# Twelve ring slots for the small experts' weight loads, and their down weights read in runs of 8192 bytes

## The chip, the cores and the metric

The kernel runs on one core of a Trainium2 chip. The metric is the device time of one execution in microseconds (us); the time before is the median of three runs. Five engines work side by side: TensorE (PE; its weight loads are listed apart as PEld), VectorE (DVE), ScalarE (ACT), GpSimd (POOL) and SyncE (SP), which here issues nearly all transfers. The transfers run on 16 DMA engines of the core.

## The reference

Two layers of a backbone over 256 latent and 256 context tokens of width 1024. Each has a mixer of three parallel head groups; the first ends in a dense SwiGLU, the second in a mixture of eight experts, of which each token takes two. Only that last part matters here:

```
def swiglu(h, wg, wu, wd):
    return (jax.nn.silu(h @ wg) * (h @ wu)) @ wd

def moe_swiglu(h, w_router, wg, wu, wd):            # h (256, 1024), wg, wu (8, 1024, 3584), wd (8, 3584, 1024)
    logits = (t @ w_router).astype(jnp.float32)
    top_v, top_i = lax.top_k(logits, TOP_K)         # TOP_K = 2
    top_w = jax.nn.softmax(top_v, axis=-1)
    gates = jnp.sum(jax.nn.one_hot(top_i, N_EXPERTS) * top_w[..., None], axis=1)
    for e in range(N_EXPERTS):
        y = y + gates[:, e:e + 1] * swiglu(t, wg[e], wu[e], wd[e])
```

Every weight is fp32 and is read once: an expert has three matrices of 14.7 MB, eight experts 352 MB. After the experts come the residual sum and one RMSNorm whose result is the output.

## The kernel before, in words

The mixers and the dense SwiGLU come first. Then the experts run one after the other, `e` = 0 to 7, ordered by how many tokens chose them. The first four (`expert`) hold up to 128 tokens each and multiply in three float32r products: each weight tile is split by ACT and DVE into a high part `eh` (L804) and a low part `el` (L805). The last four, the small experts (`expert_small`, L1235), hold up to 64 tokens and multiply their fp32 weights as they were loaded, with no split.

A small expert goes through its 3584 hidden columns in four chunks of 896 (`FB`; `NB` = 4). One chunk has twelve loads, each a tile of up to 1 MB (128 partitions by up to 2048 fp32):

- eight of gate and up weights, in four pairs (L1268): 256 rows by 896 columns, 896 KB, in runs of 3584 bytes;
- four of down weights (L1257), of the chunk before: three of 256 rows by 1024 columns, one of 128 rows. Row `r0 + k*128 + p` of the matrix goes to partition `p`, so a run is one row, 4096 bytes.

After each pair PE multiplies (L1274; the halves of the columns for gate and up stand in different partitions of `ps`). After the eighth load ACT and DVE make `g = silu(gate) * up` (L1284, L1285); in the next chunk PE transposes `g` seven times, 128 columns at a time (`g_Ts`, L1246), and multiplies it with the down weights into `pd` (L1261). At the end of an expert (`t1`, L1298, which runs inside the next expert's first chunk) `pd` is scaled by DVE (L1313), sent back to its tokens by four products (`py`, L1318) and added to `xtk` (L1322).

Where a load goes is set by a ring of tiles ("slots"): `slot32` (L1066) takes the next name of `ring`, drops a name for good once the load's number has passed its `until`, and puts the name at the end. In the small experts five names are left: `w`, `c`, `r0`, `r1`, `r2`. SP issues the loads in program order, one `dma_start` each (L1232), and holds each until the slot's last reader on PE is done, so at most five loads are under way or waiting to be read. The order of the instructions on each engine is set by a scheduler when the kernel is built; `tc.keep_in_program_order` pins one.

Tiles that the change uses: `mpr` (two buffers each for the tags `wh` and `wl`) and `mpc` (one each) hold the split parts `eh` and `el` of the big experts, whose last two tiles are split within the first small chunk; `xeL1` holds the low part of the tokens of experts 0 and 1. `pgu` is the PSUM pool of `ps`, tags `pg` and `pu`, of two banks each; `pmt` has two banks that the transposes and `py` share.

The last expert gets `end=square` (L1389): after its additions DVE and ACT compute the squares' sums and `x * g_final` (L1337), and `finish` (L1343) scales and stores the result.

```
    ring = ["w", "c", "r0", "r1", "xh", "xl", "xt", "y", "r2", "xc"]                              # L913
    until = {"xc": 36, "xt": 42, "y": 42, "xh": 62, "xl": 62}                                     # L914
    nm = ring.pop(0)                                                                              # L1070
    while i >= until.get(nm, i + 1):                                                              # L1071
```

Of the kernel before, what the change touches and what calls it, by code (L numbers as in the profile page):

```python
# [11 lines left out]
F32 = mybir.dt.float32  # L12
# [8 lines left out]
P = 128  # L21
# [70 lines left out]
def hybrid_backbone_kernel(  # L92
# [41 lines left out]
    def bank(pool, name):  # L134
        return pool.tile([P, 512], F32, tag="b", name=name)
# [754 lines left out]
    for k in range(KD):  # L890
# [13 lines left out]

    slots = {"w": lambda: mpw.tile([P, 2048], F32, tag="w32", name="e32"),
             "c": lambda: mpc.tile([P, 2048], F32, tag="w32", name="e32"),
             "xh": lambda: mp.tile([P, 2048], F32, tag="xeH0", name="e32"),
             "xl": lambda: mp.tile([P, 2048], F32, tag="xeL0", name="e32"),
             "xt": lambda: mp2.tile([P, 2048], F32, tag="xtk", name="e32"),
# [88 lines left out]
    def half(ap):  # L998
        return ap.rearrange("p (a n) -> p a n", n=NL)
# [226 lines left out]
    def load_raw(dram, kk, n):  # L1226
        i = n_load[0]
        n_load[0] += 1
        w32 = slot32(i)
        assert len(w32.shape) == 2  # L1230
        wv = w32[:, :kk * n].rearrange("p (k n) -> p k n", n=n)
        nc.sync.dma_start(wv, dram)  # L1232
        return wv

    def expert_small(xs, wg, wu, wd, e, tail, hooks, end=None):  # L1235
        H = P // 2
        xv = xs[:, :, (e - NBIG) * H:(e - NBIG + 1) * H]
        pd = [None]

        HB = FB // 2  # L1240
        NB = FE // FB

        def g_Ts(g):
            pt = bank(pmt, "pgt")
            for q in range(FK):
                nc.tensor.transpose(pt[:, q * H:(q + 1) * H], g[0:H, q * P:(q + 1) * P], ident[0:H, 0:H])  # L1246
            gt = mp2.tile([P, FK, H], F32, tag="gts", name="gts")
            copy_bal(gt, pt[:, 0:FK * H].rearrange("p (q n) -> p q n", n=H))
            return gt

        def down_s(gt, j):
            if pd[0] is None:
                pd[0] = pdn.tile([P, 512], F32, tag=f"pd{e % 2}", name="pds")
            for q0 in range(0, FK, 2):
                kn = min(2, FK - q0)
                r0 = j * FB + q0 * P
                w = load_raw(wd[r0:r0 + kn * P, :].rearrange("(k p) n -> p k n", p=P), kn, D)  # L1257
                for k in range(kn):
                    q = q0 + k
                    for o in range(2):  # L1260
                        mm(pd[0][H * o:H * o + H, :], lhsT=gt[:, q, :], rhs=w[:, k, o * 512:(o + 1) * 512],  # L1261
                           start=j == 0 and q == 0, stop=j == NB - 1 and q == FK - 1, skip_group_check=True)

        prev = None
        for j in range(NB):
            ps = pgu.tile([P, 2, 512], F32, tag=("pg", "pu")[j % 2], name="pgs")
            for c in range(KD // 2):
                ws = [load_raw(w_ap[c * 256:(c + 1) * 256, j * FB:(j + 1) * FB].rearrange("(k p) n -> p k n", p=P), 2, FB)  # L1268
                      for w_ap in (wg, wu)]
                for k in range(2):  # L1270
                    kk = 2 * c + k
                    for b in range(2):
                        for o in range(2):
                            mm(ps[H * o:H * o + H, b, 0:HB], lhsT=xv[:, kk, :], rhs=ws[o][:, k, b * HB:(b + 1) * HB],  # L1274
                               start=kk == 0, stop=kk == KD - 1, skip_group_check=True)
                if c == 1:
                    if prev is not None:
                        gt = g_Ts(prev)
# [12 lines left out]
            for f in (hooks or {}).get(j, ()):  # L1291
                f()
        last = []

        def t0():
            last.append(g_Ts(prev))

        def t1():  # L1298
            if end:
                tc.keep_in_program_order(nc.scalar.preload_act_table_set(LN_EXP))  # L1300
                new_xg()
            down_s(last[0], NB - 1)
            pt = bank(pmt, "pst")
            for t in range(2):
                nc.tensor.transpose(pt[:, t * P:(t + 1) * P], f32(S[:, t, e, :]), ident)
            for t in range(2):
                mm(pt[:, 256:257], lhsT=f32(S[:, t, e, :]), rhs=gatp[:, t, e:e + 1], start=t == 0, stop=t == 1)
            ST = mp2.tile([P, 256], F32, tag="ST", name="STs", bufs=2)
            nc.vector.tensor_copy(ST, pt[:, 0:256])
            gs = mp.tile([P, 1], F32, tag="gs", name="gs", bufs=2)  # L1310
            nc.vector.tensor_copy(gs, pt[:, 256:257])
            yo = part(y32, e % 2)
            stt(yo, half(pd[0]), gs, ga2s, op0=ALU.mult, op1=ALU.mult)  # L1313
            for t in range(2):
                pys = []
                for o in range(2):
                    py = bank(pmt, "py")
                    mm(py, lhsT=ST[H * o:H * o + H, t * P:(t + 1) * P], rhs=yo[H * o:H * o + H], start=True, stop=True)  # L1318
                    pys.append(py)
                for o in range(2):  # L1320
                    cs = slice(o * 512, (o + 1) * 512)
                    tt(xtk[:, t, cs], xtk[:, t, cs], pys[o], ALU.add)  # L1322
            if end:
                for o in range(2):
                    end(o)
        return t0, t1

    xg = None
# [5 lines left out]
    ssq4 = mp.tile([P, 2, 2], F32, name="ssq4")  # L1334
    junk = xT[:, 4:6, 0:NL]

    def square(o):  # L1337
        for t in range(2):
            xo = half(xtk[:, t, o * 512:(o + 1) * 512])
            act(junk, xo, AF.Square, accum_out=ssq4[:, t, o:o + 1])  # L1340
            tt(half(xg[:, t, o * 512:(o + 1) * 512]), xo, part(gfb, o), ALU.mult)

    def finish():  # L1343
        tt(ssq, ssq4[:, :, 0], ssq4[:, :, 1], ALU.add)
# [37 lines left out]
    for e in range(NE):  # L1382
        if e == 0:
            ws = [w[0, 0] for w in (wm_g, wm_u, wm_d)]
        else:
            ws = [w[0, ds(which[e], 1)].rearrange("o a b -> (o a) b") for w in (wm_g, wm_u, wm_d)]
        hooks = {j: f for (ee, j), f in plan.items() if ee == e}
        if e >= NBIG:
            tail = expert_small(xes[NBIG], *ws, e, tail, hooks, square if e == NE - 1 else None)  # L1389
            continue  # L1390
        xe, h = (x01, e * P) if e < 2 else (xes[2], (e - 2) * P)
        xv = (xe[0][:, :, h:h + P], xe[1][:, :, h:h + P])
        gt_ = gates if e == 0 else gatp
        tail = expert(xv, *ws, lambda t, e=e: S[:, t, e, :], lambda t, e=e, g=gt_: g[:, t, e:e + 1], tail, hooks, e == 0)
    tail[0]()
    tail[1]()
    finish()

    cv = nc.values_load(cnti[0:1, 0:1], min_val=0, max_val=NL)
    with tc.If(cv > 0):  # L1400
        pc = mp3.tile([P, 2], F32, name="pc")
        gc = mp3.tile([P, 2], F32, name="gc")
        bc = mp3.tile([P, 1], F32, name="bc")
        S2 = mp3.tile([P, 2, P], F32R, name="S2")
        xe2 = xe_tiles(1)
        for blk in range(2):
            with tc.For_i(0, NE, 1) as ei:
                nc.vector.tensor_copy(pc, posm[:, :, ds(ei, 1)].rearrange("p t o -> p (t o)"))
                nc.vector.tensor_copy(gc, gates[:, :, ds(ei, 1)].rearrange("p t o -> p (t o)"))
                nc.vector.tensor_copy(bc, base[:, ds(ei, 1)])  # L1410
                ts_(pc, pc, bc, float(P * blk), op0=ALU.subtract, op1=ALU.subtract)
# [8 lines left out]
        for o in range(2):  # L1420
            square(o)
        finish()


# [29 lines left out]
```

## Time and profile before

| | |
|---|---|
| median of 3 runs | 1977.64 us (1975.27 to 1979.37) |
| the profiled execution | 1976.52 us, of which its span is 1974.7 us |
| PE busy | 1816.8 us, 92% |
| PEld busy | 1259.1 us, 64% |
| DVE busy | 979.2 us, 50% |
| ACT busy | 758.7 us, 38% |
| read from memory | 477.39 MB, 242 GB/s over the span |

The shares are means over stages with different limits. The page shows the span in 40 slices of 49.4 us; the small experts are the last ten or so. There PE is busy eight tenths of the time and DVE hardly at all, while the DMA engines stand at nine tenths or more. A DMA share is the mean busy share of the 16 engines; a packet counts as busy from its start to its end, and packets can overlap, so a share can come out a little over 1.

### The profile page before, as it was taken

To read this page: it belongs to the slowest core of one execution; us is meant where nothing else is said; L and a number is where in the kernel's file an instruction comes from. 1 tells how busy PE (TensorE), PEld (TensorE's weight loads), DVE (VectorE), ACT (ScalarE), POOL (GpSimd) and SP (SyncE) were. 2 spreads that over 40 slices of the span, in tenths; PEclk is the share of its full clock that TensorE was granted. 3 is DMA by queue.
4 is the path that set the end of the run, shared out by engine and by line. 5 is a ranking of instruction groups with operands and counts; after the bars stand their busy time and mean duration, and the time that the engine had idled before them with its cause. 6 is when DMAs were issued, how large, how long until landed. Compare 5 with 4: busy or idle time off the path is not lost.

```text
span 1974.7 us, 23529 instructions
## 1 busy us (share of the span) xinstructions
PE 1816.8 (92%) x9280; PEld 1259.1 (64%) x9280; DVE 979.2 (50%) x1294; ACT 758.7 (38%) x965; POOL 46.7 (2%) x75
## 2 busy tenths in 40 slices
PE   7998999999999999999899999999998878887876
PEld 4756766778877887777687878888785322222222
DVE  5474555633333345755678888988984101010101
ACT  3424454422222224345566777777662000000001
POOL 1030000000000000210000000000000000000000
PEclk8999999999999999999989999999999999999998
DMA  8765243342334334553489789999998999999996
GB/s 281 223 178 143 70 132 100 115 144 70 101 99 156 110 108 155 158 140 128 146 298 360 255 305 330 334 356 361 353 340 317 366 388 388 388 382 402 396 397 249
DMA packets 261922, 480.05 MB, mean 243 GB/s; under 512 B 11630, under 2 KB 141996, under 8 KB 261804
## 3 DMA queue, kind: packets, MB, share of 16 engines
q1 hardware_dynamic: 259296, 474.19, 67.8%
q0 software_dynamic: 1312, 2.62, 0.9%
q10 hardware_dynamic: 1196, 1.66, 0.3%
q8 instruction: 75, 1.23, 0.3%
q14 instruction: 43, 0.35, 0.1%
HBM read 477.39 MB, written 1.05 MB: 242 GB/s over the span
## 4 chain that ended last, share of the span: by engine, by line
PE 74%; DMA 15%; DVE 7%; ACT 3%; issue 2%; SPq 0%; POOL 0%; DVEq 0%; ACTq 0%; POOLq 0%
DMA e<-in_w_moe_up_dram 10%; PE pd L1146 8%; PE pgs L1274 6%; DMA e<-in_w_moe_down_dram 3%; PE pu L152 3%; PE pg L151 3%; PE pu L153 3%; PE pg L152 3%; PE pu L151 3%; PE pg L153 2%; PE pds L1261 2%; PE psg L151 2%; PE psu L151 2%; PE psu L152 2%; PE psu L153 2%; PE psd L151 2%
## 5 line engine op out<-in xcount | busy, mean ns | idle before, releaser
L805 DVE TENSOR_TENSOR el<-e,eh 128x2048 fp32r<-128x2048 f32 (+1 forms) x173 | 375.4, 2189 | 49.5 <-ACT eh L804 48.8
L804 ACT ACTIVATE eh<-e 128x2048 fp32r<-128x2048 f32 (+1 forms) x173 | 316.7, 1839 | 93.1 <-PE pu L153 32.7
L1274 PE MATMUL pgs<-e,xs 128*64 128x448 f32 x1024 | 228.7, 557 | 71.1 <-DMA e<-in_w_moe_up_dram 64.4
L1274 PEld LDWEIGHTS pgs<-e,xs 128*64 128x64 f32 x1024 | 75.6, 138 | 218.7 <-DMA e<-in_w_moe_up_dram 105.0
L144 ACT ACTIVATE wh<-w 128x2048 fp32r<-128x2048 f32 (+2 forms) x70 | 125.4, 1791 | 208.4 <-issue 80.0
L145 DVE TENSOR_TENSOR wl<-w,wh 128x2048 fp32r<-128x2048 f32 (+2 forms) x70 | 149.6, 2138 | 97.9 <-ACT wh L144 97.9
L1285 DVE TENSOR_TENSOR es<-es,pgs 64x448 f32<-64x448 f32 x32 | 19.9, 623 | 324.0 <-ACT es L1284 324.0
L1284 ACT ACTIVATE es<-pgs 64x448 f32<-64x448 f32 x32 | 17.2, 537 | 325.6 <-PE pgs L1274 315.2
L1261 PE MATMUL pds<-e,gts 128*64 128x512 f32 x448 | 109.6, 599 | 9.9 <-DMA e<-in_w_moe_down_dram 9.0
L151 PE MATMUL pg<-eh,xeH 128*128 128x512 f32 x224 | 89.7, 400 | 0.6 <-ACT eh L804 0.6
L151 PE MATMUL psp<-hH,wh 128*128 128x512 f32 (+1 forms) x224 | 86.7, 391 | 3.1 <-ACT hH L276 3.0
L152 PE MATMUL pg<-el,xeH 128*128 128x512 f32 x224 | 89.4, 399 | 0.0
L151 PE MATMUL pu<-eh,xeH 128*128 128x512 f32 x224 | 88.8, 397 | 0.0
L152 PE MATMUL pu<-el,xeH 128*128 128x512 f32 x224 | 88.2, 394 | 0.7 <-DVE el L805 0.6
L151 PE MATMUL psq<-wh,hH 128*128 128x256 f32 x304 | 88.5, 291 | 0.0
L153 PE MATMUL pg<-eh,xeL 128*128 128x512 f32 x224 | 88.5, 395 | 0.0
L152 PE MATMUL psq<-wl,hH 128*128 128x256 f32 x304 | 87.7, 289 | 0.0
L153 PE MATMUL pu<-eh,xeL 128*128 128x512 f32 x224 | 87.7, 391 | 0.0
L153 PE MATMUL psq<-wh,hL 128*128 128x256 f32 x304 | 87.4, 287 | 0.0
L152 PE MATMUL psp<-hL,wh 128*128 128x512 f32 (+1 forms) x224 | 86.1, 384 | 0.0
L153 PE MATMUL psp<-hH,wl 128*128 128x512 f32 (+1 forms) x224 | 85.6, 383 | 0.0
L1261 PEld LDWEIGHTS pds<-e,gts 128*64 128x64 f32 x448 | 32.0, 136 | 68.6 <-issue 39.0
(504 smaller groups left out, 3470.8 us busy)
## 6 DMA issues: line engine op xcount, KB each, us to landing
e<-in_w_moe_down_dram SPq DMA_DIRECT2D x103, 1024.0 KB, 7.9
e<-in_w_moe_gate_dram SPq DMA_DIRECT2D x64, 896.0 KB, 7.8
e<-in_w_moe_up_dram SPq DMA_DIRECT2D x64, 896.0 KB, 7.1
e<-in_w_moe_gate_dram SPq DMA_DIRECT2D x55, 1024.0 KB, 7.3
e<-in_w_moe_up_dram SPq DMA_DIRECT2D x55, 1024.0 KB, 6.5
wmod<-in_w_mod_dram SPq DMA_DIRECT2D x96, 512.0 KB, 5.7
w<-in_w_in_dram SPq DMA_DIRECT2D x24, 1024.0 KB, 8.0
w<-in_w_ffn_gate_dram SPq DMA_DIRECT2D x11, 1024.0 KB, 5.8
```

The costliest lines, as they stand in the source:

```text
L144: act(wh[:, :m], w32[:, :m], AF.Copy)
L145: tt(wl[:, :m], w32[:, :m], f32(wh[:, :m]), ALU.subtract)
L151: mm(ps, lhsT=sh, rhs=mh, start=first, stop=False)
L152: mm(ps, lhsT=sh, rhs=ml, start=False, stop=False)
L153: mm(ps, lhsT=sl, rhs=mh, start=False, stop=last)
L804: act(h3[:, b], w[:, b], AF.Copy)
L805: tt(l3[:, b], w[:, b], f32(h3[:, b]), ALU.subtract)
L1146: mm(pds[o], lhsT=gt[sh][:, q, :], rhs=w[mh][:, k, o * 512:(o + 1) * 512], start=a and j == 0 and q == 0, stop=z and j == NJ - 1 and q == 3)
L1261: mm(pd[0][H * o:H * o + H, :], lhsT=gt[:, q, :], rhs=w[:, k, o * 512:(o + 1) * 512], start=j == 0 and q == 0, stop=j == NB - 1 and q == F ...
L1274: mm(ps[H * o:H * o + H, b, 0:HB], lhsT=xv[:, kk, :], rhs=ws[o][:, k, b * HB:(b + 1) * HB], start=kk == 0, stop=kk == KD - 1, skip_group_c ...
L1284: act(gv, ps[0:H, b, 0:HB], AF.Silu)
L1285: tt(gv, gv, ps[H:P, b, 0:HB], ALU.mult)
```

## The change

The ring gets seven more names as the first small expert (`e == NBIG`) starts its second chunk: the two buffers of each of `wh` and `wl` in `mpr`, the two of `mpc`, and `xeL1`. Ring order then is the five old names and the seven new ones. Within the down weights' loads a partition now takes seven rows in sequence (row `p*7 + k` of the chunk), so two rows are one run of 8192 bytes in memory; the fourth load, with one row, keeps 4096. The columns of `g` are transposed in the matching order, every seventh column. In the last expert the four products `py` go to the `pgu` banks, and the additions come before the products with `g_final`. After the experts the ring goes back to five names for code that does not run with these inputs.

```
--- before.py
+++ after.py
@@ -904,6 +904,11 @@
 
     slots = {"w": lambda: mpw.tile([P, 2048], F32, tag="w32", name="e32"),
              "c": lambda: mpc.tile([P, 2048], F32, tag="w32", name="e32"),
+             "mh": lambda: mpr.tile([P, 2048], F32, tag="wh", name="e32"),
+             "ml": lambda: mpr.tile([P, 2048], F32, tag="wl", name="e32"),
+             "ch": lambda: mpc.tile([P, 2048], F32, tag="wh", name="e32"),
+             "cl": lambda: mpc.tile([P, 2048], F32, tag="wl", name="e32"),
+             "xm": lambda: mp.tile([P, 2048], F32, tag="xeL1", name="e32"),
              "xh": lambda: mp.tile([P, 2048], F32, tag="xeH0", name="e32"),
              "xl": lambda: mp.tile([P, 2048], F32, tag="xeL0", name="e32"),
              "xt": lambda: mp2.tile([P, 2048], F32, tag="xtk", name="e32"),
@@ -1243,7 +1248,7 @@
         def g_Ts(g):
             pt = bank(pmt, "pgt")
             for q in range(FK):
-                nc.tensor.transpose(pt[:, q * H:(q + 1) * H], g[0:H, q * P:(q + 1) * P], ident[0:H, 0:H])
+                nc.tensor.transpose(pt[:, q * H:(q + 1) * H], g.rearrange("p (n k) -> p k n", k=FK)[0:H, q], ident[0:H, 0:H])
             gt = mp2.tile([P, FK, H], F32, tag="gts", name="gts")
             copy_bal(gt, pt[:, 0:FK * H].rearrange("p (q n) -> p q n", n=H))
             return gt
@@ -1253,8 +1258,7 @@
                 pd[0] = pdn.tile([P, 512], F32, tag=f"pd{e % 2}", name="pds")
             for q0 in range(0, FK, 2):
                 kn = min(2, FK - q0)
-                r0 = j * FB + q0 * P
-                w = load_raw(wd[r0:r0 + kn * P, :].rearrange("(k p) n -> p k n", p=P), kn, D)
+                w = load_raw(wd[j * FB:(j + 1) * FB, :].rearrange("(p k) n -> p k n", k=FK)[:, q0:q0 + kn], kn, D)
                 for k in range(kn):
                     q = q0 + k
                     for o in range(2):
@@ -1263,6 +1267,8 @@
 
         prev = None
         for j in range(NB):
+            if e == NBIG and j == 1:
+                ring.extend(["mh", "ml", "mh", "ml", "ch", "cl", "xm"])
             ps = pgu.tile([P, 2, 512], F32, tag=("pg", "pu")[j % 2], name="pgs")
             for c in range(KD // 2):
                 ws = [load_raw(w_ap[c * 256:(c + 1) * 256, j * FB:(j + 1) * FB].rearrange("(k p) n -> p k n", p=P), 2, FB)
@@ -1311,18 +1317,20 @@
             nc.vector.tensor_copy(gs, pt[:, 256:257])
             yo = part(y32, e % 2)
             stt(yo, half(pd[0]), gs, ga2s, op0=ALU.mult, op1=ALU.mult)
+            keep = tc.keep_in_program_order if end else lambda i: i
+            pys = {}
+            if end:
+                spare = [pgu.tile([P, 2, 512], F32, tag=tag, name="py") for tag in ("pg", "pu")]
             for t in range(2):
-                pys = []
                 for o in range(2):
-                    py = bank(pmt, "py")
+                    py = spare[o][:, t] if end else bank(pmt, "py")
                     mm(py, lhsT=ST[H * o:H * o + H, t * P:(t + 1) * P], rhs=yo[H * o:H * o + H], start=True, stop=True)
-                    pys.append(py)
+                    pys[t, o] = py
                 for o in range(2):
                     cs = slice(o * 512, (o + 1) * 512)
-                    tt(xtk[:, t, cs], xtk[:, t, cs], pys[o], ALU.add)
+                    keep(tt(xtk[:, t, cs], xtk[:, t, cs], pys[t, o], ALU.add))
             if end:
-                for o in range(2):
-                    end(o)
+                end()
         return t0, t1
 
     xg = None
@@ -1334,11 +1342,14 @@
     ssq4 = mp.tile([P, 2, 2], F32, name="ssq4")
     junk = xT[:, 4:6, 0:NL]
 
-    def square(o):
+    def squares():
         for t in range(2):
-            xo = half(xtk[:, t, o * 512:(o + 1) * 512])
-            act(junk, xo, AF.Square, accum_out=ssq4[:, t, o:o + 1])
-            tt(half(xg[:, t, o * 512:(o + 1) * 512]), xo, part(gfb, o), ALU.mult)
+            for o in range(2):
+                act(junk, half(xtk[:, t, o * 512:(o + 1) * 512]), AF.Square, accum_out=ssq4[:, t, o:o + 1])
+        for t in range(2):
+            for o in range(2):
+                cs = slice(o * 512, (o + 1) * 512)
+                tc.keep_in_program_order(tt(half(xg[:, t, cs]), half(xtk[:, t, cs]), part(gfb, o), ALU.mult))
 
     def finish():
         tt(ssq, ssq4[:, :, 0], ssq4[:, :, 1], ALU.add)
@@ -1386,7 +1397,7 @@
             ws = [w[0, ds(which[e], 1)].rearrange("o a b -> (o a) b") for w in (wm_g, wm_u, wm_d)]
         hooks = {j: f for (ee, j), f in plan.items() if ee == e}
         if e >= NBIG:
-            tail = expert_small(xes[NBIG], *ws, e, tail, hooks, square if e == NE - 1 else None)
+            tail = expert_small(xes[NBIG], *ws, e, tail, hooks, squares if e == NE - 1 else None)
             continue
         xe, h = (x01, e * P) if e < 2 else (xes[2], (e - 2) * P)
         xv = (xe[0][:, :, h:h + P], xe[1][:, :, h:h + P])
@@ -1395,6 +1406,7 @@
     tail[0]()
     tail[1]()
     finish()
+    ring[:] = [nm for nm in ring if nm in ("w", "c", "r0", "r1", "r2")]
 
     cv = nc.values_load(cnti[0:1, 0:1], min_val=0, max_val=NL)
     with tc.If(cv > 0):
@@ -1417,8 +1429,7 @@
                 for f in expert(xv, sq_(wm_g), sq_(wm_u), sq_(wm_d), lambda t: S2[:, t, :], lambda t: gc[:, t:t + 1], None):
                     f()
         new_xg()
-        for o in range(2):
-            square(o)
+        squares()
         finish()
```

The same build order shows on SP in what a load waits for, from the fourth load of the second chunk of the first small expert. `DMAHW0` to `DMAHW7` are eight counters that the loads of the queue take in turn; a load that waits for one waits until the load named has landed. `PE` and `DVE` stand for the last reader of the slot. The row `ISA` ahead of each load is left out. Before:

```order
L1232 DMA e_11821<-in_w_moe_up_dram 128x2x896 [waits DMAHW3_49,DVE_49]
...
L1232 DMA e_11841<-in_w_moe_gate_dram 128x2x896 [waits DMAHW4_49,DVE_49]
...
L1232 DMA e_11843<-in_w_moe_up_dram 128x2x896 [waits DMAHW5_49,PE_49]
...
L1232 DMA e_11855<-in_w_moe_up_dram 128x2x896 [waits DMAHW7_49,PE_49]
...
L1232 DMA e_11871<-in_w_moe_down_dram 128x2x1024 [waits DMAHW0_49,PE_49]
...
L1232 DMA e_11894<-in_w_moe_gate_dram 128x2x896 [waits DMAHW4_49,PE_49]
```

The same loads in the changed kernel:

```order
L1237 DMA e_11821<-in_w_moe_up_dram 128x2x896 [waits DMAHW3_49,DVE_49]
...
L1237 DMA e_11841<-in_w_moe_gate_dram 128x2x896 [waits DMAHW4_49,DVE_49]
...
L1237 DMA e_11843<-in_w_moe_up_dram 128x2x896 [waits DMASW4_49,DMASW3_49,DMASW5_49,DMASW2_49,DMASW6_49,DMASW1_49,DMASW7_49,DMASW0_49,PE_49]
...
L1237 DMA e_11855<-in_w_moe_up_dram 128x2x896 [waits PE_49]
...
L1237 DMA e_11871<-in_w_moe_down_dram 128x2048 [waits DMAHW5_49]
...
L1237 DMA e_11894<-in_w_moe_gate_dram 128x2x896 [waits DMAHW1_49,PE_49]
```

The sixth load (`e_11843`) is the first that goes to a new slot: there PE is the reader of the big experts' tile that was in it. The ninth (`e_11871`, now one run of 2048 elements for each partition) waits for no reader on PE any more, but for the counter of the load eight places before it. From the thirteenth on (`e_11894`) a load waits for that counter and for the reader of its slot twelve places before.

On DVE at the end of the last expert, the additions to `xtk`, the products `xg` with `g_final` and the first step of `finish`. Before:

```order
L1313 SCALAR_TENSOR_TENSOR xT<-pds,gs,xT 128x2x256 [waits DVE_49,PE_49]
L1322 TENSOR_TENSOR xtk<-xtk,py 128x512 [waits PE_49]
L1341 TENSOR_TENSOR xg<-xtk,xT 128x512 [waits DVE_49]
L1322 TENSOR_TENSOR xtk<-xtk,py 128x512 [waits PE_49] x2
L1341 TENSOR_TENSOR xg<-xtk,xT 128x512 [waits DVE_49]
L1322 TENSOR_TENSOR xtk<-xtk,py 128x512 [waits PE_49]
L1341 TENSOR_TENSOR xg<-xtk,xT 128x512 [waits DVE_49] x2
L1344 TENSOR_TENSOR ssq<-ssq_7907 128x2 [waits Activation_49]
```

The same place in the changed kernel:

```order
L1319 SCALAR_TENSOR_TENSOR xT<-pds,gs,xT 128x2x256 [waits DVE_49,PE_49]
L1331 TENSOR_TENSOR xtk<-xtk,py 128x512 [waits PE_49] x4
L1352 TENSOR_TENSOR xg<-xtk,xT 128x512 [waits DVE_49] x4
L1355 TENSOR_TENSOR ssq<-ssq_7907 128x2 [waits Activation_49]
L1365 TENSOR_SCALAR xg<-xg,ssq 128x512 [waits DVE_49,Activation_49]
```

The same eight instructions stand between the scaling of `pd` and the sum of squares, the four additions now first. On PE and ACT every instruction stands where it stood.

## Rows read from the trace of the kernel before

**Rows 1.** The page: DMA share and GB/s in 40 slices, two queues.
```profile
DMA  8765243342334334553489789999998999999996
GB/s 281 223 178 143 70 132 100 115 144 70 101 99 156 110 108 155 158 140 128 146 298 360 255 305 330 334 356 361 353 340 317 366 388 388 388 382 402 396 397 249
...
q1 hardware_dynamic: 259296, 474.19, 67.8%
...
q8 instruction: 75, 1.23, 0.3%
```

**Rows 2.** Chain of waits in a small expert: start us, us, what.
```profile
1553.52 8.15 DMA e<-in_w_moe_up_dram
...
1561.71 2.50 PE pgs L1274 x12
...
1564.23 6.44 DMA e<-in_w_moe_up_dram
```

**Rows 3.** SP's own waits, 1527 to 1955 us: us, times, longest.
```profile
SPq L1232 <- PE pgs L1274: 225.3, 76, 10.0
SPq L1232 <- PE pds L1261: 82.2, 59, 3.3
```

**Rows 4.** Stretches: busy us of each engine, PE clock, DMA share, GB/s.
```profile
1400.00:1430.00 30.00, 30.00 (x135) 24.20 (x134) 27.22 (x17) 21.56 (x14) 0.00 (x0) 1.00 1.01 366
...
1525.00:1530.00 5.00, 5.00 (x21) 2.42 (x20) 1.72 (x3) 0.94 (x2) 0.00 (x0) 1.00 0.36 145
1530.00:1535.00 5.00, 5.00 (x18) 1.93 (x16) 2.67 (x5) 0.32 (x1) 0.00 (x0) 1.00 0.13 20
1535.00:1550.00 15.00, 13.54 (x71) 5.84 (x72) 2.19 (x4) 1.62 (x3) 0.00 (x0) 1.00 1.00 389
1550.00:1590.00 40.00, 32.28 (x157) 11.79 (x157) 2.56 (x4) 2.22 (x4) 0.00 (x0) 1.00 1.03 406
1650.00:1655.00 5.00, 3.42 (x18) 1.10 (x16) 0.00 (x0) 0.00 (x0) 0.00 (x0) 1.00 1.03 416
...
1527.00:1955.50 428.50, 341.18 (x1585) 120.42 (x1583) 41.62 (x70) 23.61 (x42) 0.00 (x0) 0.99 0.99 384
1955.00:1960.00 5.00, 3.56 (x18) 1.07 (x16) 0.75 (x1) 0.00 (x0) 0.00 (x0) 1.00 0.10 42
```

**Rows 5.** Timeline: PE's last big-expert products, and SP's loads around them.
```profile
1522.64 0.37 SPq L1232 DMA_DIRECT2D e<-in_w_moe_gate_dram  x1
...
1524.37 0.65 PE L1146 MATMUL pd<-eh,gth 128*128 128x512 f32 x2
...
1527.81 0.63 PE L1146 MATMUL pd<-eh,gtl 128*128 128x512 f32 x2
...
1533.24 0.37 SPq L1232 DMA_DIRECT2D e<-in_w_moe_up_dram  x1
```

**Rows 6.** Groups of PE, 1527 to 1956 us: busy us, mean ns | idle.
```profile
L1274 PE MATMUL pgs<-e,xs 128*64 128x448 f32 x958 | 213.9, 558 | 68.4 <-DMA e<-in_w_moe_up_dram 61.7 <-DMA e<-in_w_moe_gate_dram 5.2 <-ACT gts L289 1.4
L1261 PE MATMUL pds<-e,gts 128*64 128x512 f32 x438 | 107.4, 599 | 9.9 <-DMA e<-in_w_moe_down_dram 9.0 <-DVE gts L291 0.7
...
L1246 PEld LDWEIGHTS pgt<-ident,es 64*128 64x128 f32 x112 | 8.9, 138 | 18.5 <-DVE es L1285 14.9 <-issue 3.6
```

**Rows 7.** Timeline of the end: DVE's and ACT's last work before `finish`.
```profile
1960.59 0.69 DVE L1322 TENSOR_TENSOR xtk<-xtk,py 128x512 f32<-128x512 f32 x1 [1.22 <-PE py L1318]
...
1964.42 1.28 DVE L1341 TENSOR_TENSOR xg<-xtk,xT 128x512 f32<-128x512 f32 x2
...
1964.80 0.63 ACT L1340 ACTIVATE xT<-xtk 128x512 f32<-128x512 f32 x1
...
1965.62 0.15 DVE L1344 TENSOR_TENSOR ssq<-ssq 128x2 f32<-128x2 f32 x1
```

More of the change, by code (lines that the diff above doesn't have):

```diff
@@ L906, in hybrid_backbone_kernel @@
              "c": lambda: mpc.tile([P, 2048], F32, tag="w32", name="e32"),
+             "mh": lambda: mpr.tile([P, 2048], F32, tag="wh", name="e32"),
+             "ml": lambda: mpr.tile([P, 2048], F32, tag="wl", name="e32"),
+             "ch": lambda: mpc.tile([P, 2048], F32, tag="wh", name="e32"),
+             "cl": lambda: mpc.tile([P, 2048], F32, tag="wl", name="e32"),
+             "xm": lambda: mp.tile([P, 2048], F32, tag="xeL1", name="e32"),
              "xh": lambda: mp.tile([P, 2048], F32, tag="xeH0", name="e32"),
@@ L1245, in g_Ts @@
             for q in range(FK):
-                nc.tensor.transpose(pt[:, q * H:(q + 1) * H], g[0:H, q * P:(q + 1) * P], ident[0:H, 0:H])
+                nc.tensor.transpose(pt[:, q * H:(q + 1) * H], g.rearrange("p (n k) -> p k n", k=FK)[0:H, q], ident[0:H, 0:H])
             gt = mp2.tile([P, FK, H], F32, tag="gts", name="gts")
@@ L1255, in down_s @@
                 kn = min(2, FK - q0)
[L1256 to L1257 removed]
+                w = load_raw(wd[j * FB:(j + 1) * FB, :].rearrange("(p k) n -> p k n", k=FK)[:, q0:q0 + kn], kn, D)
                 for k in range(kn):
@@ L1265, in expert_small @@
         for j in range(NB):
+            if e == NBIG and j == 1:
+                ring.extend(["mh", "ml", "mh", "ml", "ch", "cl", "xm"])
             ps = pgu.tile([P, 2, 512], F32, tag=("pg", "pu")[j % 2], name="pgs")
@@ L1313, in t1 @@
             stt(yo, half(pd[0]), gs, ga2s, op0=ALU.mult, op1=ALU.mult)
+            keep = tc.keep_in_program_order if end else lambda i: i
+            pys = {}
+            if end:
+                spare = [pgu.tile([P, 2, 512], F32, tag=tag, name="py") for tag in ("pg", "pu")]
             for t in range(2):
-                pys = []
                 for o in range(2):
-                    py = bank(pmt, "py")
+                    py = spare[o][:, t] if end else bank(pmt, "py")
                     mm(py, lhsT=ST[H * o:H * o + H, t * P:(t + 1) * P], rhs=yo[H * o:H * o + H], start=True, stop=True)
-                    pys.append(py)
+                    pys[t, o] = py
                 for o in range(2):
                     cs = slice(o * 512, (o + 1) * 512)
-                    tt(xtk[:, t, cs], xtk[:, t, cs], pys[o], ALU.add)
+                    keep(tt(xtk[:, t, cs], xtk[:, t, cs], pys[t, o], ALU.add))
             if end:
-                for o in range(2):
-                    end(o)
+                end()
         return t0, t1
@@ L1335, in hybrid_backbone_kernel, with squares @@
     junk = xT[:, 4:6, 0:NL]
-    def square(o):
+    def squares():
         for t in range(2):
-            xo = half(xtk[:, t, o * 512:(o + 1) * 512])
-            act(junk, xo, AF.Square, accum_out=ssq4[:, t, o:o + 1])
-            tt(half(xg[:, t, o * 512:(o + 1) * 512]), xo, part(gfb, o), ALU.mult)
+            for o in range(2):
+                act(junk, half(xtk[:, t, o * 512:(o + 1) * 512]), AF.Square, accum_out=ssq4[:, t, o:o + 1])
+        for t in range(2):
+            for o in range(2):
+                cs = slice(o * 512, (o + 1) * 512)
+                tc.keep_in_program_order(tt(half(xg[:, t, cs]), half(xtk[:, t, cs]), part(gfb, o), ALU.mult))
     def finish():
@@ L1388, in hybrid_backbone_kernel @@
         if e >= NBIG:
-            tail = expert_small(xes[NBIG], *ws, e, tail, hooks, square if e == NE - 1 else None)
+            tail = expert_small(xes[NBIG], *ws, e, tail, hooks, squares if e == NE - 1 else None)
             continue
@@ L1397, in hybrid_backbone_kernel @@
     finish()
+    ring[:] = [nm for nm in ring if nm in ("w", "c", "r0", "r1", "r2")]
     cv = nc.values_load(cnti[0:1, 0:1], min_val=0, max_val=NL)
@@ L1419, in hybrid_backbone_kernel @@
         new_xg()
-        for o in range(2):
-            square(o)
+        squares()
         finish()
```

## The prediction

> **What bounds the kernel now.** I read the page's 40 slices first [rows 1]: in the last ten or so the DMA engines are at nine tenths and more and move 382 to 402 GB/s. That looks full, but a share counts a packet as busy while it waits, so the next view is the stretches [rows 4]. Where the loads flow, as in 1550 to 1590 us, the rate is 406 GB/s at a share of 1.03. Over the whole stretch from 1527 to 1955.5 us it is 384 GB/s at 0.99, and after 1527 us it falls to nearly nothing for 7 us (145 GB/s in the five us around it, then 20). So there are holes. The chain of waits says what they are made of [rows 2]: 6 to 8 us of a load, then 2.5 us of PE's products, then a load again. A load waits for PE to read out its slot, and PE waits for that load. SP's own waits add it up [rows 3]: in 428 us SP stood 225.3 us for PE's gate and up products and 82.2 us for its down products, 307.5 us in 135 waits. A load that needs 5 to 8 us from issue to landing is started only when one of five slots is free, so few are under way at once. PE itself is busy 341.2 of the 428.5 us, at a granted clock of 0.99 of the 2.4 GHz level [rows 4]; it is not the bound. The small experts are bound by the transfers, at a pace 5% under the one that the same transfers reach with more of them queued.
>
> **The change part by part.** All of it acts from the second chunk of the first small expert.
>
> *Seven slots more.* Loads are numbered here within that chunk. The first five go to the old slots, as before; before, the sixth waits until PE has read the first, and SP issues it at 1533.24 us, 10.6 us after the fifth [rows 5]. In the changed order the sixth waits for the reader of a big expert's split tile. PE's products with the first of these two tiles end by 1525.0 us, with the second by 1528.4 us [rows 5], so loads six and seven can go at about 1525 and eight to twelve at about 1528.5. That closes the hole: load five keeps the engines busy till about 1527 us. From then on a load waits for the landing of the load eight places before it and for a slot used twelve places before. Up to eight can be under way, and PE may fall behind by four more before a load is held up.
>
> What is left to move from load six on: 128 gate and up loads less 13 are 115 of 896 KB, 48 down loads of 1024 KB and 16 of 512 KB, in all 164.2 MB (384 GB/s over 428.5 us gives 164.5, so the count holds). At 406 GB/s that is 404.4 us, against 428.5 us: **24.1 us** saved. I take 406 because it is a mean over 40 us with loads of every kind; the ends are 391 GB/s, which the stretch after 1535 us reaches as it is (164.5 MB less 0.2 over 420.5 us), and 416, the best five us seen [rows 4].
>
> A queue that starts from nothing needs a moment, and not every slow piece need come from an empty queue. Nothing shows a queue eight deep, so I bound this from both sides: 0, or 0.6 us at the start (15 us at 389 instead of 406 [rows 4]) and some few us more over the stretch. I take **2.0 us** lost.
>
> The eight counters are a new wait. What is queued behind a load held by one is the next load on SP; with seven others under way the engines have over 6 MB, 15 us of work, so it costs nothing. If loads landed out of order it could cost up to a load's 2.3 us at a time.
>
> *Runs of 8192 bytes.* Three loads per chunk go from 256 packets to 128: 384 packets less per chunk, 24 per engine, 384 per engine over 16 chunks. What one packet costs apart from its bytes follows from two rows. The main queue's 259296 packets took 67.8% of 16 engines over 1974.7 us, 82.6 ns each, at 474.19 MB / 259296 = 1829 bytes [rows 1]. In 1550 to 1590 us a packet has 3740 bytes on the mean (2048 of 3584 and 896 of 4096 per chunk) and takes 1.03 x 16 x 3740 / 406 = 151.8 ns [rows 4]. The line through both has 0.0362 ns per byte and 16 ns per packet. With the big experts' stretch instead (2458 bytes, 1.01 x 16 x 2458 / 366 = 108 ns [rows 4]) it is 25 ns. So the saving lies between 0, should longer runs be cut up again, and 384 x 25 = 9.7 us; I take 16 ns, since that row covers the whole execution: **6.3 us**. No row of this queue has a packet over 4096 bytes, and the other end is a rival below.
>
> *Strided transposes.* 112 weight loads of `g` on PE, 138 ns each and the same as contiguous ones of other tiles, now read every seventh fp32 [rows 6]. No row shows a strided weight load. PE's cover is large: 341.2 us busy, some 13 us of waits for ACT and DVE, against about 398 us of transfers, so 44 us or 0.4 us for each transpose before PE is late. I take nothing, and price the rest below. The Trainium skill, "SBUF — State Buffer", section on the DMA port swizzle, says that SBUF has 16-byte lines, that each access to a new line pays a penalty, and that fp32 can therefore stride by four for nothing. By that rule a step of seven costs up to four times as much, an estimate of 0.41 us more for each load, 46 us of PE in all, which would use up the cover and no more; no run here shows it yet, and it speaks against a part of the change that I cost at nothing.
>
> *The end.* After the last load DVE does eight instructions between 1960.59 and 1965.62 us, one behind the other, and only then the sum of squares; ACT's last square starts at 1964.80 [rows 7]. The change puts the additions first but leaves all eight ahead of that sum on DVE, so squares that are ready sooner wait for DVE: 0, with bounds of 0.7 us (one instruction) either way.
>
> The sum goes against the profiled execution's 1976.5 us: less 24.1, less 6.3, plus 2.0, is 1948.1 us. The median of the three runs is 1.1 us over the profiled one, so I forecast **1949 us**.
>
> **The rivals.**
>
> *The holes are the transfers' own.* If 391 GB/s is what these loads get with the queue full, only the hole after 1527 us goes: 164.2 MB / 391 = 420 us, 8.5 us saved, and packets that then wait for memory rather than for their own cost save nothing: 1976.5 + 1.1 - 8.5 = 1969 us. For it: shares are 0.99 to 1.03 nearly everywhere. Against: rates drop where SP waits, and 406 is held for 40 us.
>
> *The deeper queue also lifts the pace.* At the best row's 416 GB/s, 164.2 MB take 394.7 us: 33.8 saved by slots, 6.3 by packets, 2.0 lost, 1939.5 us. Against it: that row is five us right after a hole. The Trainium skill, "DMA: Bandwidth & Descriptors", section Bandwidth, gives 425 GB/s for one 16 MB transfer; by that figure alone the slots would save an estimated 42 us, and no stretch of this trace reaches it.
>
> *Long runs are slow (slower than before).* The one queue with large packets, of instructions, has 75 of 16.4 KB that took 0.3% of 16 engines, 1264 ns each or 77 ns per KB, against 41 ns per KB of the weights [rows 1, 4]. It writes elsewhere, so it says little. But at that price an 8192-byte run takes 630 ns where two of 4096 take 332: 384 x 0.30 = 115 us more, less 22 for the slots, 2071 us. It decides from 57 ns per run (22 us / 384) upward. Rows 28 KB apart in memory could do a little of this too; gate and up rows are 14 KB apart and run at the full 406.
>
> *The strided transposes make PE the bound.* At seven times 138 ns, if every word passed over is read as well, each costs 0.83 us more, 93 us: PE with its waits needs 447 us, past the 428.5 of before, so 19 us slower, 1996 us. Up to 0.66 us more per transpose the kernel is still faster than before.
>
> **How the numbers follow.** Forecast 0.70; holes stay 0.12; higher pace 0.09; long runs slow 0.05; PE the bound 0.04. The range must reach from the higher pace to the holes that stay: 1940 to 1969 us, which leaves out the last two and about half of the third, 0.14. What this kernel's timing can tell from no change is about 0.2%, 4 us. The first three cases lie beyond it: 0.91 faster. Of the last two a third would come out near zero: 0.03 the same, 0.06 slower.
>
> **What would show it.** In the changed profile: SP issuing loads six to twelve of that chunk between 1525 and 1531 us, and no piece under 380 GB/s from there to the last load; its waits on PE small, on landings (the counters) large; the last load landing near 1928 instead of 1955 us; the main queue with some 6100 packets fewer, and about 410 GB/s in stretches (the sum's 398 to 400 us). PE's busy time about as before, with transposes of 138 ns. It is wrong if the rate stays near 390 with SP no longer waiting for PE, if the down loads run slower than gate and up, or if PE's idle time before its products goes while the end does not come earlier.

## The result, and the profile after

The changed kernel takes 1952.91 us (median of 5 runs, 1951.22 to 1953.75), beside 1979.37 us for the kernel before (5 runs, 1975.27 to 1985.6). The ratio is 0.9873 (95% interval 0.9845 to 0.9901), or some 25 us; a second set (`again`, below) gave 0.9891 (0.9873 to 0.9909). The forecast of 1949 us was 4 us low, inside its range of 1940 to 1969.

The page of the changed kernel, same lines as [rows 1]:

```profile
DMA  9665232343234244564289798999998999999996
GB/s 287 224 179 146 71 129 88 99 145 106 82 108 151 87 132 136 162 161 141 66 306 355 264 320 316 353 327 354 350 353 321 394 410 411 410 410 409 410 410 258
...
q1 hardware_dynamic: 253152, 474.19, 67.8%
```

The last slices stand at 409 to 411 GB/s, where they ran from 382 to 402. The main queue has 259296 - 253152 = 6144 packets fewer: a run of 8192 bytes is one packet. The stretches, columns as in [rows 4]:

```profile
1525.00:1530.00 5.00, 5.00 (x17) 3.03 (x16) 0.00 (x0) 0.00 (x0) 0.00 (x0) 0.88 1.00 364
1530.00:1535.00 5.00, 5.00 (x20) 1.74 (x20) 3.88 (x6) 1.26 (x2) 0.00 (x0) 1.00 0.96 359
...
1527.00:1930.00 403.00, 336.05 (x1580) 127.19 (x1580) 41.63 (x70) 23.61 (x42) 0.00 (x0) 0.99 1.02 409
...
1920.00:1930.00 10.00, 8.39 (x44) 3.48 (x42) 2.15 (x5) 1.82 (x2) 0.00 (x0) 1.00 0.93 384
...
1930.00:1935.00 5.00, 4.93 (x24) 1.35 (x20) 0.02 (x1) 0.00 (x0) 0.00 (x0) 1.00 0.15 60
```

The hole after 1527 us is gone (145 and 20 GB/s before), though 1525 to 1535 us, at 364 and 359, stay under the 380 GB/s that the prediction named as a sign. Over the whole stretch the rate is 409 GB/s, and it falls off at the end: 384 over the last ten us of it. Counted at the full rate, the 60 GB/s of the last row are 0.7 us of transfer, so by this count the loads end at about 1930.7 us, and before at about 1955.5. The last packets come a little later, at about 1932.6 and before at 1956.4 us. The DMA share of the stretch is 1.02, where it was 0.99.

What SP waits for, 1527 to 1930 us, beside [rows 3]:

```profile
SPq L1237 <- PE pds L1265: 62.9, 39, 2.4
SPq L1237 <- DMA e<-in_w_moe_up_dram: 59.1, 42, 3.2
SPq L1237 <- DMA e<-in_w_moe_gate_dram: 48.3, 32, 1.7
SPq L1237 <- PE pgs L1280: 23.4, 35, 3.4
```

Before, SP stood 307.5 us for PE's products; now 86.3 us, and 107.4 us for landings of gate and up loads, which are the eight counters (down loads add 13.3 us, other instructions of PE 24.2). While SP stands in a wait for a counter seven other loads are under way, and the rate of 409 GB/s shows no loss by it. How many are under way also shows in the time from issue to landing of the gate loads (loads, KB each, median us). Before:

```profile
e<-in_w_moe_gate_dram SPq DMA_DIRECT2D x64, 896.0 KB, 7.8
```

After:

```profile
e<-in_w_moe_gate_dram SPq DMA_DIRECT2D x64, 896.0 KB, 17.0
```

896 KB take 2.4 us at 384 GB/s and 2.2 us at 409, so as an estimate three loads were under way before and seven to eight are now. SP's loads around the hole, to be read beside [rows 5]:

```profile
1524.35 0.37 SPq L1237 DMA_DIRECT2D e<-in_w_moe_gate_dram  x1
1526.31 0.37 SPq L1237 DMA_DIRECT2D e<-in_w_moe_up_dram  x1
1526.89 0.37 SPq L1237 DMA_DIRECT2D e<-in_w_moe_gate_dram  x1
1530.23 0.37 SPq L1237 DMA_DIRECT2D e<-in_w_moe_up_dram  x1
1530.79 2.07 SPq L1237 DMA_DIRECT2D e<-in_w_moe_down_dram  x4
```

Load five goes out at 1524.35 us, load six 2 us later (10.6 us before), and twelve by 1532.9. The forecast was 1525 to 1531 us; load five itself is 1.7 us later than before.

### The profile page after: what moved, and what is told of

Its sections match the earlier page's. It is cut to its first block, busy times and chain, and to the rows that moved or that the text cites. A ratio compares the mean times of both kernels' runs of the same rounds, so it can differ in the third digit from the quotient of the medians.

```text
span 1951.1 us, 23538 instructions
## 1 busy us (share of the span) xinstructions
PE 1814.2 (93%) x9280; PEld 1267.4 (65%) x9280; DVE 979.4 (50%) x1294; ACT 758.6 (39%) x965; POOL 46.6 (2%) x75
## 3 DMA queue, kind: packets, MB, share of 16 engines
q1 hardware_dynamic: 253152, 474.19, 67.8%
## 4 chain that ended last, share of the span: by engine, by line
PE 72%; DMA 16%; DVE 7%; ACT 3%; issue 2%; SPq 0%; POOL 0%; DVEq 0%; ACTq 0%; POOLq 0%
DMA e<-in_w_moe_up_dram 11%; PE pd L1151 8%; PE pgs L1280 3%; DMA e<-in_w_moe_down_dram 3%; PE pu L152 3%; PE pg L151 3%; PE pu L153 3%; PE pg L152 3%; PE pu L151 3%; PE pg L153 3%; PE pds L1265 2%; PE psg L151 2%; PE psg L152 2%; PE psg L153 2%; PE psu L152 2%; PE psu L151 2%
## 5 line engine op out<-in xcount | busy, mean ns | idle before, releaser
L1280 PE MATMUL pgs<-e,xs 128*64 128x448 f32 x1024 | 222.8, 552 | 51.3 <-DMA e<-in_w_moe_up_dram 51.3
L1151 PE MATMUL pd<-eh,gth 128*128 128x512 f32 x224 | 71.2, 400 | 2.6 <-ACT eh L804 2.4
```

Of the source, the lines that this page charges most:

```text
L1151: mm(pds[o], lhsT=gt[sh][:, q, :], rhs=w[mh][:, k, o * 512:(o + 1) * 512], start=a and j == 0 and q == 0, stop=z and j == NJ - 1 and q == 3)
```

## The experiments

All compare with the kernel before on the same chip. The rate and SP's waits for PE's products (gate and up, and down, added) are those of the stretch from 1560 to 1900 us in each run's trace.

| run | slots | runs of down weights | transposes | ratio to before (95%) | GB/s | SP for PE, us |
|---|---|---|---|---|---|---|
| before | 5 | 4096 | contiguous | 1 | 393 | 247 |
| runs_only | 5 | 8192 | strided | 1.0026 (1.0011 to 1.0042) | 393 | 251 |
| runs_again | 5 | 8192 | strided | 0.9995 (0.9979 to 1.0011) | 384 | 254 |
| runs_contig | 5 | 8192 | contiguous | 0.9983 (0.9963 to 1.0003) | 397 | 251 |
| strides_only | 5 | 4096 | strided | 1.0022 (1.0008 to 1.0036) | 392 | 247 |
| ring6 | 6 | 4096 | contiguous | 0.9938 (0.9920 to 0.9955) | 403 | 246 |
| ring8 | 8 | 4096 | contiguous | 0.9898 (0.9876 to 0.9920) | 407 | 229 |
| ring_only | 12 | 4096 | contiguous | 0.9899 (0.9873 to 0.9925) | 407 | 120 |
| after_contig | 12 | 8192 | contiguous | 0.9889 (0.9866 to 0.9912) | 410 | 77 |
| again (the change) | 12 | 8192 | strided | 0.9891 (0.9873 to 0.9909) | 410 | 78 |
| early8 | 8, from the first chunk | 8192 | strided | 0.9871 (0.9849 to 0.9892) | 409 | 235 |
| early12 | 12, three from the first chunk | 8192 | strided | 0.9842 (0.9824 to 0.9860) | 410 | 75 |
| early12_end | as early12, end changed | 8192 | strided | 0.9845 (0.9827 to 0.9863) | 410 | 76 |

Rates and waits come from one profiled execution each. With five slots the same kernel gave 393 and 384 GB/s on two chips (`runs_only`, `runs_again`), so differences of some ten GB/s among the rows with five slots say nothing.

The theory was that the gain is the slots': loads wait for PE because few are under way. The rival tested here gives it to the long runs.

**The slots alone.** The ring's edit of the change without the rest:

```
+            if e == NBIG and j == 1:
+                ring.extend(["mh", "ml", "mh", "ml", "ch", "cl", "xm"])
```

> The seven more slots alone; down weights in runs of 4096 bytes, contiguous transposes and the old end stay. If the slots carry the gain: SP hardly waits for PE any more, the stretch from 1527 us to the last load runs at 405 to 407 GB/s, and the kernel is 20 to 23 us faster than before (ratio 0.988 to 0.990). Rival, that the long runs set the changed kernel's pace and the slots only fill the hole after 1527 us: the stretch stays at 390 to 395 GB/s and the gain is 8 to 10 us (ratio 0.995 to 0.996).

Ratio 0.9899, 20 us, and 406 GB/s from 1527 to 1930 us. The slots carry the gain, at the rate expected; the rival's 390 to 395 is out. But SP's waits for PE did not nearly go, as I had expected: 120 of 247 us are left, at the full rate.

```profile
1527.00:1930.00 403.00, 329.37 (x1571) 118.49 (x1571) 41.62 (x70) 23.60 (x42) 0.00 (x0) 1.00 1.03 406
...
1560.00:1900.00 340.00, 273.81 (x1304) 97.37 (x1302) 32.06 (x54) 17.82 (x33) 0.00 (x0) 1.00 1.03 407
```

**How many slots.** The same edit with `["ch", "cl", "xm"]`:

> As the run with the slots alone, but three slots more instead of seven (the two of mpc and xeL1): eight in all, as many as the counters let under way. If what counts is that a few more loads are queued than the two or three of before: 17 to 22 us faster than before (ratio 0.989 to 0.991), close to the twelve. Rival, that PE falls behind by more than a few loads and needs the rest: 8 to 13 us (ratio 0.993 to 0.996).

and with `["xm"]`:

> The slots alone again, with one more than before (xeL1), six in all; runs, transposes and end as before. The run with eight slots was as fast as the one with twelve. If a slot is worth one more load under way, as long as fewer than about four are: some 8 to 14 us faster than before (ratio 0.993 to 0.996), with SP still waiting for PE but the rate from 1527 us at 392 to 400 GB/s. Rival, that any first slot closes the holes: the whole 20 us (ratio 0.990). Other rival, that only the big experts' tiles close the hole after 1527 us: under 4 us.

Eight slots are as good as twelve: the same 407 GB/s, though SP still waits 229 us for PE. With six the ratio is 0.9938, 12 us, and the rate from 1527 us is 397 GB/s, as expected of one more load under way (403 from 1560 to 1900 us). There SP waits as long as with five, 246 against 247 us. So a wait on SP is no loss by itself; it is one when too little is left in the queue behind it.

**The long runs and the transposes, with five slots.** The edits of `down_s` and `g_Ts` alone:

```
-                nc.tensor.transpose(pt[:, q * H:(q + 1) * H], g[0:H, q * P:(q + 1) * P], ident[0:H, 0:H])
+                nc.tensor.transpose(pt[:, q * H:(q + 1) * H], g.rearrange("p (n k) -> p k n", k=FK)[0:H, q], ident[0:H, 0:H])
...
-                w = load_raw(wd[r0:r0 + kn * P, :].rearrange("(k p) n -> p k n", p=P), kn, D)
+                w = load_raw(wd[j * FB:(j + 1) * FB, :].rearrange("(p k) n -> p k n", k=FK)[:, q0:q0 + kn], kn, D)
```

> Runs of 8192 bytes and the strided transposes alone, with the five slots of before. If slots carry the gain: SP still waits some 300 us for PE, and the kernel is 1 to 4 us faster (ratio 0.998 to 0.9995), since a down load lands a little sooner. Rival, that the runs carry it: 12 us or more (ratio 0.994 or less).

It was 5 us slower, which neither theory had, though its profiled execution was no slower. So I ran it again beside its halves: `runs_contig` has the second edit alone, `strides_only` the first alone.

> The long runs and strided transposes with five slots once more, beside their two halves. The first time it took 5 us more than before (ratio 1.0011 to 1.0042), while its profile shows the small experts' stage 2 us shorter. If that was no accident: 1.001 to 1.004 again.

> Runs of 8192 bytes with five slots and contiguous transposes, so that the numbers are not the reference's. With five slots PE's time stands between two loads, so slower transposes (7 per chunk, 0.06 to 0.08 us each, 8 us in all) are paid. If they made the run with both slower: 2 to 6 us faster than before (ratio 0.997 to 0.999). Rival, that long runs themselves are worse with few loads under way: 1.001 to 1.004 as with both.

> The strided transposes alone with five slots and down weights as before, so that the numbers are not the reference's. If the transposes are paid with five slots: 4 to 9 us slower than before (ratio 1.002 to 1.0045). Rival: no change within 2 us.

The 5 us did not come back (0.9995 the second time), so a size for both together stays open between none and some 5 us. The transposes alone cost 4.3 us (1.0022, interval above 1), the low end of what was expected if PE's time stands between two loads and is paid. That rests on one set of runs, and a set of the same strength, `runs_only`, did not come back; the one trace does not show it either (392 GB/s, a span of 1971.9 against 1974.7 us before). The long runs alone tend to a gain of 3 us, but their interval holds 1. What these runs do show is that the long runs do not carry the change: the 12 us or more of the rival are out in all three sets with long runs.

The trace of `runs_only`, of PE's transposes (duration ns min, median, max):

```profile
L1246 PEld LDWEIGHTS pgt<-ident,es x105: 193/218/221, 1550.5 to 1943.8; 64*128 64x128 f32 x105
L1246 PE MATMUL pgt<-ident,es x105: 282/283/332, 1550.5 to 1943.9; 64*128 64x64 f32 x105
```

A strided weight load takes 218 ns at the median against 138, and the transpose itself 283 ns against 222.

**The transposes with twelve slots.** The changed kernel with the old line of `g_Ts`:

> The changed kernel with g transposed from contiguous columns again, so that the down products take their rows in another order than their weights: the numbers are not the reference's. If PE's cover hides the strided weight loads (137 to 218 ns, 112 of them, 9 us of PE): the same time as the changed kernel within 1 us, 24 to 27 us under before, with the weight loads back at 138 ns. Rival, that PE is on the path at the end of each chunk: 2 to 5 us faster than the changed kernel.

0.9889, some 22 us and a little under what was expected, against 0.9891 for the change on another chip. These intervals are some 4 us wide to either side, too wide to put the rival's 2 to 5 us out by themselves. The traces do: with the weight loads back at 138 ns (median), the rate is 410 GB/s as in the change, the last five us from 1930 have the same 60 GB/s, and the spans are 1951.3 and 1951.1 us. Behind a full queue PE's time is hidden here. Against `ring_only` on the same chip (0.9899) the timed runs do not tell whether the long runs and the new end give anything; only the rates do, 410 against 407 GB/s.

**Opening the ring earlier.** The trace of the changed kernel still has a hole one chunk before the first new slot is used:

```profile
1495.00:1505.00 10.00, 10.00 (x50) 5.21 (x51) 1.72 (x4) 0.60 (x1) 0.00 (x0) 1.00 0.66 211
```

```
-            if e == NBIG and j == 1:
-                ring.extend(["mh", "ml", "mh", "ml", "ch", "cl", "xm"])
+            if e == NBIG and j == 0:
+                ring[:] = ["xm"] + [nm for nm in ring if nm in ("w", "c", "r0", "r1", "r2")] + ["ch", "cl"]
+            if e == NBIG and j == 1:
+                ring.extend(["mh", "ml", "mh", "ml"])
```

> The changed kernel once more, beside the next two on the same chip: 23 to 28 us faster than before (ratio 0.986 to 0.9885).

> The changed kernel with three of its seven slots (xeL1 and the two of mpc) in the ring from the first chunk of the first small expert on, the four of mpr from the second as they were. Before the change the rate falls to 213 and 166 GB/s between 1495 and 1505 us, and PE waits 6.5 us for a load at 1505 and 3.7 us for one more and its split at 1515. If that hole is of the same kind as the others: those ten us stay at 380 GB/s or more, and the kernel is 4 to 7 us faster than the changed one. Rival, that DVE and ACT, which split the big experts' last tiles, hold the chunk whatever is loaded: the same within 2 us.

`again` gave 0.9891, some 21.5 us, a little under the 23 to 28 expected. With the ring opened earlier it is 1944.86 us against 1955.20 on the same chip: 10 us faster than the change, more than the 4 to 7 expected, and 0.9842 of before. In its trace, the hole and the stretch after:

```profile
1495.00:1505.00 10.00, 10.00 (x47) 5.69 (x46) 2.50 (x2) 0.00 (x0) 0.00 (x0) 1.00 1.01 382
1505.00:1520.00 15.00, 11.47 (x55) 4.79 (x54) 4.61 (x7) 5.16 (x5) 0.00 (x0) 0.89 1.03 405
1520.00:1535.00 15.00, 15.00 (x52) 7.82 (x52) 7.16 (x9) 1.26 (x2) 0.00 (x0) 0.88 1.03 414
```

In the trace of the changed kernel the same three stretches run at 211, 387 and 362 GB/s; what more is moved here is worth, as an estimate at 410 GB/s, 6 to 7 us. The span here is 5.7 us shorter than in that trace and 9.1 us shorter than in that of `again`. The rest of the 10 us is not placed.

Without the four tiles of `mpr` (the last two lines of the edit dropped):

> The changed kernel with three slots from the first small chunk on and none of mpr: eight in all. Twelve from there on gave 0.9842 of before, eight from the second chunk on was as good as twelve. If four to five loads under way are all that the transfers can use: 0.983 to 0.986 again. Rival, that the four of mpr matter once the first chunk's hole is closed: 0.988 or more.

0.9871, between the two. It ran on another chip than `early12`, and the two intervals just overlap, so the timed runs alone do not settle it. The traces say where a difference would come from: the rate from 1560 us on is the same, but at the change from big to small experts a hole is back (416 GB/s in `early12`), worth 4 to 5 us by the rates. PE is then behind with the big experts' last products, and SP waits up to 9.6 us for the small experts' products that stand behind them:

```profile
1525.00:1535.00 10.00, 10.00 (x43) 3.85 (x39) 4.84 (x8) 1.26 (x2) 0.00 (x0) 1.00 0.62 232
```

SP's waits from 1505 to 1560 us, the longest group:

```profile
SPq L1237 <- PE pgs L1280: 31.4, 11, 9.6
```

So eight slots do while PE keeps pace, and by the traces the four more pay where it does not.

**The end.** On top of `early12`: two tiles in turn for the transposed `g`, one `pgu` tile for each half of the tokens, and the sum of squares ahead of two of the products:

```
-                    py = spare[o][:, t] if end else bank(pmt, "py")
+                    py = spare[t][:, o] if end else bank(pmt, "py")
...
     def finish():
-        tt(ssq, ssq4[:, :, 0], ssq4[:, :, 1], ALU.add)
+        tc.keep_in_program_order(tt(ssq, ssq4[:, :, 0], ssq4[:, :, 1], ALU.add))
+        times_g(1)
```

> As the one before it, and at the end: two tiles in turn for the transposed g, so that its copy does not wait for the products before it; the products py of one half of the tokens in one tile of pgu and of the other half in the other, so that PE does not wait for DVE between them; and the sum of squares on DVE ahead of two of the products with g_final. Each is on the path after the last load: 0.7, 0.6 and 0.9 us, in all about 2 us faster than the run before it, from the last load to the end 16 instead of 18 us. Rival, that the end is bound by the last loads and the stores: no difference.

The timed runs cannot tell it from `early12` (1944.40 and 1944.86 us, intervals alike). Nor can the spans of the profiled executions, 1942.6 against 1945.4 us, since that of `early12` was the slowest of its five. DVE's end in it:

```profile
1929.61 2.48 DVE L1333 TENSOR_TENSOR xtk<-xtk,py 128x512 f32<-128x512 f32 x4 [1.23 <-PE py L1329]
1932.01 1.28 DVE L1356 TENSOR_TENSOR xg<-xtk,xT 128x512 f32<-128x512 f32 x2
1933.35 0.16 DVE L1359 TENSOR_TENSOR ssq<-ssq 128x2 f32<-128x2 f32 x1
```

The first addition to the sum of squares is 3.7 us, where the changed kernel needs 5.5 (next section). From the scaling of `pd` to the end of the span it is 15.0 us, 16.1 in `early12`. That it makes the kernel some 1 us faster is likely from this, and not shown; about 2 us were expected.

## Why the prediction was right, and where it missed

*What bounds the kernel, and the slots.* Right. The holes were SP waiting for slots, and they closed. `ring_only` gives 406 GB/s over the whole stretch and 407 from 1560 us on. So a full queue is 1 us better than the 406 taken for it, and of the 2.0 us set aside for a slow start about 1 us was lost (364 and 359 GB/s from 1525 to 1535 us in the change). Each of these two made the forecast saving 1 us too small, while the packets (next) made it 3.4 us too large; that the three mostly cancel is luck. By the count above the loads end 24.8 us earlier, with the packets' share in it. I had put all seven slots down as needed; three give the same rate. Of the signs named, two did not come: the piece from 1525 to 1535 us is under 380 GB/s, and the transposes' weight loads take 218 ns and not 138. The rival of holes that are the transfers' own is out, since the same packets run at 406 GB/s with more slots, and so is the higher pace of 416: the stretch stays at 407, and at 410 with the long runs.

*The long runs.* Right in kind, mis-sized: 6.3 us forecast from 16 ns a packet. Between `ring_only` at 407 and the change at 410 GB/s, 164.2 MB take 403.4 and 400.5 us: 2.9 us, or 7.6 ns for each of 384 packets, inside the bounds of 0 and 9.7. `after_contig`, on the chip of `ring_only`, has the same 410. The rival of slow long runs is out by these rates. Why the line through the two rows gave too much is not shown. The rows differ in more than the size of a packet: one is a mean over the whole execution, the other a stretch of one stage. Two full queues with packets of different size, as here, are the better measure.

*The strided transposes.* Costed at nothing behind PE's cover, and that holds with twelve slots. The rival's seven times 138 ns is out. The Trainium skill's rule of the 16-byte lines ("SBUF — State Buffer", section on the DMA port swizzle) has a penalty for each access that crosses to a new line. The trace agrees that the step costs something, 218 against 138 ns, but the estimate of four times is not what was measured, which is 1.6; only one step was run, so that the lines are the reason is not shown. With five slots the same transposes cost 4 us in one set of runs; that this is PE's time between two loads is argued, not shown.

*The end.* Costed at nothing, with 0.7 us either way, and DVE's part is slightly worse than nothing. DVE in the changed kernel:

```profile
1936.95 1.29 DVE L1331 TENSOR_TENSOR xtk<-xtk,py 128x512 f32<-128x512 f32 x2 [1.21 <-PE py L1327]
1938.85 1.29 DVE L1331 TENSOR_TENSOR xtk<-xtk,py 128x512 f32<-128x512 f32 x2 [0.61 <-PE py L1327]
1940.05 2.49 DVE L1352 TENSOR_TENSOR xg<-xtk,xT 128x512 f32<-128x512 f32 x4
1942.46 0.15 DVE L1355 TENSOR_TENSOR ssq<-ssq 128x2 f32<-128x2 f32 x1
```

From the first addition to the sum of squares 5.51 us, 5.03 before [rows 7]. As forecast, the eight instructions are all ahead of the sum. But the third product `py` still waits: it goes to the other half of a `pgu` tile that DVE is reading, and the tile is released as a whole, so DVE stands idle for 0.61 us. In `early12_end`, with one tile for each half of the tokens, the four additions run without that wait. I had not seen it in the diff. From PE's last product of `pd` to the end of the span it is 16.2 us, 16.1 before, so this half microsecond does not show in the profiled execution's time.

A wait took the place of the loads there, too. After the last gate and up loads PE has more to do than the transfers:

```profile
1928.03 0.62 DVE L291 COPY gts<-pgt 128x448 f32<-128x448 f32 x1 [3.96 <-PE pds L1265]
...
1928.70 6.23 PE L1265 MATMUL pds<-e,gts 128*64 128x512 f32 x28 [0.73 <-DVE gts L291]
...
1932.13 0.20 PEld L1265 LDWEIGHTS pds<-e,gts 128*64 128x64 f32 x4 [0.66 <-DMA e<-in_w_moe_down_dram]
...
1934.98 0.75 DVE L1319 SCALAR_TENSOR_TENSOR xT<-pds,gs,xT 128x512 f32<-128x512 f32 x1 [6.33 <-PE pds L1265]
```

Before, the last twelve products waited for a load:

```profile
1955.78 2.80 PE L1261 MATMUL pds<-e,gts 128*64 128x512 f32 x12 [0.59 <-DMA e<-in_w_moe_down_dram]
```

Now all 28 products of the last chunk run in one piece, and only two of their weight loads wait for a load, 0.9 us in all. They end 2.3 us after the last packet, before 2.2. From the end of the loads as counted above (1930.7 and 1955.5 us) to the end of the span it is 20.4 us, 19.2 before; 1.0 of the difference is that the transfers tail off for longer, 1.9 us after that count against 0.9.

*The sum.* The profiled execution is 23.6 us shorter, 28.4 were forecast. Of the 4.8 us, 1.7 lie before the change acts: load five goes out at 1524.35 instead of 1522.64 us after the same instructions. It differs between executions of one kernel, 1527.71 us in `again`; what sets it is not shown. 3.4 are the packets, against which stand the 1.0 of the slow start that was not lost and the 1.0 of the better pace. 1.2 are the end, nearly all of it the transfers' tail. The remaining 0.5 us I have not placed. The median of before also came out 1.7 us higher than the one I had reckoned from.

## What to carry to other kernels

A DMA share near 1 does not say that the queue is full: compare the rate of the whole stage with the best 40 us in it, and look at what the issuing engine waits for. Where it waits for buffers, count how many loads are really under way; here going from five slots to eight gave all of the rate, and by the traces the rest only bridged the moment in which the reader was behind. With such a ring too short a small cost on the reader can show (here 4 us in one set of runs); with it long enough the same cost did not show, so such edits should be tried after the ring, not before.

## What the runs showed of the hardware

A TensorE weight load of 64 by 128 fp32 with a step of 28 bytes takes 218 ns, 138 ns contiguous, and its transpose 283 ns against 222. Doubling a packet from 4096 to 8192 bytes raised the rate of this mix from 407 to 410 GB/s. With loads of about 1 MB, five tiles to load into gave 393 GB/s over 340 us, six 403, eight and twelve 407. The kernel with five slots spreads over 1969 to 1981 us on one chip (11 runs), with twelve from the first chunk over 1942 to 1947 us (5 runs); that the short ring is the reason is not shown.
